# Sample attention gathered ahead of the sample delta rule, mixer loads reordered, last norm's sums given priority

## The chip, the cores and the metric

The kernel runs on one core of one Trainium2 chip. The metric is the time of one execution in device microseconds (us). Five engines work side by side, each through its own list of instructions in order: TensorE (PE, with its weight loads as PEld), VectorE (DVE), ScalarE (ACT), GpSimd (POOL) and SyncE (SP), which here only issues DMAs. An instruction that needs another engine's result, or a transfer, waits at the head of its engine's list, and everything behind it waits too.

## The reference, cut to what matters

One step of one layer serves a prompt of 1024 tokens and, with the same weights, eight sample sequences of four tokens each (`D_MODEL` 1024, float32 throughout):

```python
h = rmsnorm(x, norm_mix_w);  p = h @ w_in            # q,k,v | conv input | z | a | b | gate_A | gate_B
o_a = stick_breaking(q, k, v)      # 8 heads x 64; samples: 256 past keys from the paged cache and 4 new ones
o_b = gated_delta(silu(conv(u)), z, a, b, state)     # 4 heads, 128x128 state
x = x + (sigmoid(g_a) * (o_a @ w_pa) + sigmoid(g_b) * (o_b @ w_pb)) @ w_o
x = x + square(relu(rmsnorm(x, norm_mlp_w) @ w_up)) @ w_down          # D_FF = 4096
y = rmsnorm(x, norm_final_w)
```

Stick-breaking weights are `sigmoid(z_j)` times the product of `1 - sigmoid(z_i)` over the later keys i, with no softmax. For the samples the past keys and values are pages of 128 rows, found through `page_table`: two pages of keys and two of values for each of the eight sequences.

## The kernel before

Everything is kept with features on the partitions (128) and the 1056 tokens (1024 + 32) along the free axis. A float32 product is made of three passes (`dense`, L137 to L139): a high part of the weights with a high part of the data, high with low, low with high. The order of every engine's instructions is fixed when the program is built: a scheduler with a model of times picks, among what is ready, the next instruction of each engine, `tc.high_priority()` moves some forward, and the result is a static list per engine. So PE often has filler between the steps of a chain: the gate projections (`pd_g`, `proj` jobs `g0_j` and `g1_j`), which belong to no chain in this stretch.

The parts that the change touches, in order of time:

- **Sample delta rule** (tiles of pool `dk`): one step of the delta rule for the 32 sample tokens. It is one long chain: conv sums (`cs`), transposes (`dtn`), norms (`drk`, with a power taken on POOL by `rpow`, L114), decays (`pcd`), `dmt`, products with the states (`dks`, two times 64 short matmuls), three rounds of `dy`, the output and its norm (`df`, again `rpow`), and the new states (`dst`), written out by SP from L723.
- **Sample attention** (pool `bk`): for each sequence s POOL gathers two pages of keys into `kg` (L819, two buffers, so that the gather of s + 2 waits until PE has transposed s), PE transposes them (`dkt`, eight transposes) and ACT copies them to `kts`. Four sequences make a group g: scores `dsc`, sigmoid `ds`, the scan on DVE, weights back through transposes `dwt`, values `dav` (from `vg`, gathered at L833, four buffers), `om`, `dos`, `osT`. Group 1 does the same with the other four sequences.
- **Prompt attention** (`sc`, `wt`, `po`): follows; DVE's scans (`pr`) and POOL's `am` and masks feed PE.
- **Channel mixer**: `up_products` (tile `pu`) makes the hidden layer in seven products over blocks of a 2x2 split and writes the combined operands to `hc_d` in DRAM (L1308). The second matrix runs as seven products for three groups of hidden blocks (tile `pw`): for each product i and each block f of a group it needs `hc{f}_i` (264 KB, L1360) and one of the quarters `a11`, `a12`, `a21`, `a22` of `w_down` (256 KB each, L1368) or a combination of them made on DVE, each split into a high and a low part by ACT and DVE. The loads all go through SP's queue: three rounds of `hc`, then all sixteen quarters of the group.
- **Last part** (tile `pv`): the remaining hidden blocks by plain products in four stages of 264 columns (`wd` weights, `hp` hidden), added to `y`; squares of `y` are summed into `sa` (L1484), PE sums over the partitions (`pf`, L1492), POOL takes the power -0.5 (`fr`), PE transposes `y` back (`fin`), ACT and DVE scale one half each (`fo`), and SP writes the rows out. The last stage has three tiles of tokens, the others two.

Of the kernel before, what the change touches and what calls it, by code (L numbers as in the profile page):

```python
# [38 lines left out]
def hybrid_step(ctx, tc, x_prompt, x_sample, cache_k, cache_v, page_table, state_conv, state_ssm,  # L39
# [730 lines left out]
    idx = bk.tile([P, 16], I32, name="idx")  # L770
    nc.scalar.dma_start(idx, page_table.rearrange("s g -> (s g)").unsqueeze(0).to_broadcast([P, 16]))
    rowi = bk.tile([P, 16], I32, name="rowi")
    G.iota(rowi, pattern=[[0, 16]], base=0, channel_multiplier=1)
    V.tensor_scalar(idx, idx, P, None, op0=ALU.mult)
    V.tensor_tensor(idx, idx, rowi, op=ALU.add)
    ckf = cache_k[0].rearrange("n t h d -> (n t) (h d)")
    cvf = cache_v[0].rearrange("n t h d -> (n t) (h d)")

# [32 lines left out]
    vgs = {}  # L811
    for g in range(2):
        psc = ttile(f"dsc{g}")
        kts = []
        for s4 in range(4):
            s = 4 * g + s4
            kg = bk.tile([P, 2, 512], F32, tag="kg", name=f"kg{s}", bufs=2)
            for pg in range(2):
                G.indirect_dma_start(kg[:, pg, :], None, ckf, bass.IndirectOffsetOnAxis(ap=idx[:, 2 * s + pg:2 * s + pg + 1], axis=0))  # L819
            kt = bk.tile([P, 4, 260], F32, tag="kts", name=f"kts{s}", bufs=6)  # L820
            for p2 in range(2):
                pt = (gtile if p2 else dtile)(f"dkt{s}_{p2}")
                for q in range(4):
# [2 lines left out]
                S_.activation(kt[:, 2 * p2:2 * p2 + 2, 0:256], pt.rearrange("p (a f) -> p a f", a=2), AF.Copy)
            V.tensor_copy(kt[:, :, 256:260], ksT[:, :, 4 * s:4 * s + 4])
            kts.append(kt)
        for s4 in range(4):
            s = 4 * g + s4  # L830
            vgs[s] = vk.tile([P, 2, 512], F32, tag="vg", name=f"vg{s}", bufs=4)
            for pg in range(2):
                G.indirect_dma_start(vgs[s][:, pg, :], None, cvf, bass.IndirectOffsetOnAxis(ap=idx[:, 2 * s + pg:2 * s + pg + 1], axis=0))  # L833
# [702 lines left out]
```

## Time and profile before

| | us |
|---|---|
| median of three runs (lowest, highest) | 1775.74 (1774.68, 1777.79) |
| the profiled execution | 1775.13 |
| its span, first to last recorded instruction | 1773.2 |
| outside the span | 1.93 |

| stage by PE's tiles | from, to (us) |
|---|---|
| gate projections used as filler (`pd_g`) | 464.2 to 765.7 |
| key pages transposed (`dkt`) | 548.3 to 643.7 |
| scores of the prompt attention (`sc`) | 681.4 to 879.1 |
| first matrix of the mixer, last matmul of `pu` | 1410.8 |
| second matrix, seven products (`pw`), first matmul | 1416.3 |
| `pv`, end | 1763.0 |
| last instruction of a compute engine, end | 1769.9 |

PE is busy for 1710.3 us of the span (96%), DVE 65%, ACT 44%, POOL 12%. Busy means that an instruction was running by the record; an instruction that waits at the head of its list is idle time of its engine, with the releaser named. "issue" as releaser means that the engine waited for nothing the profile shows. PEclk is the granted TensorE clock, 1.00 being full speed.

### The profile page before, as it was taken

The numbers are of one execution on the slowest core, as the hardware profiler recorded it, in microseconds if no ns is written. First come the engines' busy times: TensorE is split into PE (matmuls) and PEld (weight loads), VectorE is DVE, ScalarE is ACT, GpSimd is POOL, SyncE is SP. The second block draws the span as 40 slices with busy tenths as digits, with TensorE's granted clock in tenths as the row PEclk, the third lists the DMA queues.
The fourth block names the chain that finished last, engine by engine and source line by source line (L and its number), as shares of the span: only waits on it lengthen the run. The fifth ranks groups of instructions, "written<-read, shape, count | busy, mean of one in ns | idle before, by whom it ended". The sixth has DMA issues, their size and how long they took to land.

```text
span 1773.2 us, 34494 instructions
## 1 busy us (share of the span) xinstructions
PE 1710.3 (96%) x13884; PEld 1646.6 (93%) x13884; DVE 1156.5 (65%) x2312; ACT 785.3 (44%) x1563; POOL 205.0 (12%) x239
## 2 busy tenths in 40 slices
PE   7999999999999889999899999999999899999998
PEld 6999999999999668977789999999999899999998
DVE  6665777767234213677947577877777778788853
ACT  5553444343323223566523445555445555434454
POOL 1120111110001322356500000000000000000000
PEclk9999999999999889999999999999999999999999
DMA  5142232234335546578323544645444684432421
GB/s 175 43 119 77 56 115 78 90 104 145 113 106 153 181 133 160 143 186 231 125 96 121 163 145 134 171 140 149 148 141 134 216 303 146 156 112 94 135 84 75
DMA packets 233579, 239.22 MB, mean 135 GB/s; under 512 B 22754, under 2 KB 192067, under 8 KB 233420
## 3 DMA queue, kind: packets, MB, share of 16 engines
q1 hardware_dynamic: 229110, 228.40, 42.2%
q0 software_dynamic: 2560, 8.39, 1.5%
q8 instruction: 109, 1.79, 0.4%
q10 hardware_dynamic: 1750, 0.23, 0.1%
q14 instruction: 50, 0.41, 0.1%
HBM read 163.21 MB, written 73.77 MB: 134 GB/s over the span
## 4 chain that ended last, share of the span: by engine, by line
PE 70%; issue 12%; POOL 6%; DVE 6%; DMA 4%; ACT 1%; SPq 0%; POOLq 0%; DVEq 0%; ACTq 0%; another core or an unknown queue 0%
PE pu L139 6%; PE pu L137 6%; PE pu L138 6%; PE pw L138 5%; PE pw L137 5%; PE pw L139 5%; POOL am L909 3%; POOL s L906 2%; PE px L138 1%; PE px L139 1%; PE pv L137 1%; PE px L137 1%; PE pv L139 1%; PE pv L138 1%; PE pd_g L137 1%
## 5 line engine op out<-in xcount | busy, mean ns | idle before, releaser
L137 PE MATMUL pu<-Xh,uh 128*128 128x264 f32 x812 | 229.8, 283 | 1.0 <-ACT uh L1135 1.0
L139 PE MATMUL pu<-Xh,ul 128*128 128x264 f32 x812 | 230.1, 284 | 0.0
L138 PE MATMUL pu<-Xl,uh 128*128 128x264 f32 x812 | 229.7, 283 | 0.0
L137 PE MATMUL pw<-hc,w 128*128 128x264 f32 x728 | 206.7, 286 | 5.2 <-ACT w L1382 5.2
L138 PE MATMUL pw<-hc,w 128*128 128x264 f32 x728 | 207.0, 287 | 0.0
L139 PE MATMUL pw<-hc,w 128*128 128x264 f32 x728 | 201.7, 284 | 0.0
L137 PEld LDWEIGHTS pu<-Xh,uh 128*128 128x128 f32 x812 | 153.1, 189 | 1.2 <-ACT uh L1135 1.2
L138 PEld LDWEIGHTS pu<-Xl,uh 128*128 128x128 f32 x812 | 152.7, 188 | 0.0
L138 PE MATMUL pd_g<-xl,wh_g 128*128 128x256 f32 (+1 forms) x512 | 149.0, 291 | 3.2 <-issue 3.2
L139 PEld LDWEIGHTS pu<-Xh,ul 128*128 128x128 f32 x812 | 152.0, 188 | 0.0
L137 PE MATMUL pd_g<-xh,wh_g 128*128 128x256 f32 (+1 forms) x512 | 149.8, 293 | 1.4 <-issue 0.8
L139 PE MATMUL pd_g<-xh,wl_g 128*128 128x256 f32 (+1 forms) x512 | 149.9, 293 | 0.3 <-issue 0.3
L137 PEld LDWEIGHTS pw<-hc,w 128*128 128x128 f32 x728 | 137.8, 189 | 5.4 <-ACT w L1382 5.4
L138 PEld LDWEIGHTS pw<-hc,w 128*128 128x128 f32 x728 | 137.5, 189 | 0.0
L139 PEld LDWEIGHTS pw<-hc,w 128*128 128x128 f32 x728 | 135.4, 188 | 0.0
L913 DVE TENSOR_TENSOR_SCAN pr<-am 128x127 f32<-128x127 f32 (+7 forms) x64 | 89.8, 1403 | 43.0 <-POOL am L909 42.9
L138 PEld LDWEIGHTS pd_g<-xl,wh_g 128*128 128x128 f32 x512 | 97.6, 191 | 7.4 <-issue 7.1
L137 PEld LDWEIGHTS pd_g<-xh,wh_g 128*128 128x128 f32 x512 | 97.6, 191 | 6.2 <-issue 4.8
L139 PEld LDWEIGHTS pd_g<-xh,wl_g 128*128 128x128 f32 x512 | 97.5, 190 | 4.8 <-issue 4.6
L1382 ACT ACTIVATE w<-a 128x512 fp32r<-128x512 f32 x78 | 43.4, 623 | 94.3 <-PE pw L139 88.5
L114 POOL TENSOR_TENSOR fr<-fr,powc 128x3 f32<-128x3 f32 x4 | 3.4, 858 | 679.0 <-DVE fr L1493 643.2
L139 PE MATMUL px<-mh,wl_wo 128*128 128x264 f32 x256 | 72.7, 287 | 1.3 <-DVE wl_wo L1136 1.2
(581 smaller groups left out, 5198.7 us busy)
## 6 DMA issues: line engine op xcount, KB each, us to landing
hc_d<-t SPq DMA_DIRECT2D x26, 924.0 KB
hc<-hc_d SPq DMA_DIRECT2D x91, 264.0 KB
a<-in_w_down_dram SPq DMA_DIRECT2D x52, 256.0 KB
ws_g<-in_w_in_dram SPq DMA_DIRECT2D x16, 512.0 KB
ws_wo<-in_w_o_dram SPq DMA_DIRECT2D x32, 256.0 KB
ua<-in_w_up_dram SPq DMA_DIRECT2D x16, 512.0 KB
ub<-in_w_up_dram SPq DMA_DIRECT2D x16, 512.0 KB
gA_d<-gt SPq DMA_DIRECT2D x8, 528.0 KB
```

The source lines that it names most:

```text
L114: G.tensor_tensor(out, in_, powc[: out.shape[0], which:which + 1].to_broadcast([out.shape[0], n]), op=ALU.pow)
L137: PE.matmul(pt[:, :n], lhsT=wh[k], rhs=xh[k], start=(k == 0), stop=False)
L138: PE.matmul(pt[:, :n], lhsT=wh[k], rhs=xl[k], start=False, stop=False)
L139: PE.matmul(pt[:, :n], lhsT=wl[k], rhs=xh[k], start=False, stop=(k == nk - 1))
L906: G.affine_select(s[:, qsl], s[:, qsl], pattern=[[-1, P]], compare_op=ALU.is_gt, fill=0.0, base=0, channel_multiplier=1)
L909: G.tensor_scalar(am[:, :n], s[:, :n], -1.0, 1.0, op0=ALU.mult, op1=ALU.add)
L913: V.tensor_tensor_scan(pr[:, n - 1:0:-1], am_r, am_r, 1.0, op0=ALU.mult, op1=ALU.bypass)
L1382: S_.activation(tl[:, 0], src, AF.Copy)
```

## The change

**Sample attention.** The table of row numbers (`idx`) and the gathers of keys and values come from two helpers, `keys(s)` and `values(s)`. For the first four sequences they are called before the delta rule's code, for the other four inside the loop of group 1. The transposes use PSUM tiles of one kind (`dtile`, two buffers) and no longer of two; `kts` has four buffers and not six, `ds` one and not two; the pool `vk` is gone, `vg` lives in `bk`.

POOL's list, before, from the mask of the delta rule to the first mask of the prompt attention. L819 rows are gathers of keys, L833 of values, two gathers to a row; `drk` and `df` are the delta rule's powers:

```order
L819 DMA kg_6126<-in_cache_k_dram,idx 128x512 x2
L819 DMA kg_6143<-in_cache_k_dram,idx 128x512 x2
L114 TENSOR_TENSOR drk<-drk_4352,powc 128x1
L114 TENSOR_TENSOR df<-df,powc 128x1
L819 DMA kg_6160<-in_cache_k_dram,idx 128x512 x2
L819 DMA kg_6177<-in_cache_k_dram,idx 128x512 x2
L833 DMA vg_6194<-in_cache_v_dram,idx 128x512 x2
L833 DMA vg_6197<-in_cache_v_dram,idx 128x512 x2
L833 DMA vg_6200<-in_cache_v_dram,idx 128x512 x2
L833 DMA vg_6203<-in_cache_v_dram,idx 128x512 x2
L819 DMA kg_6264<-in_cache_k_dram,idx 128x512 x2
L819 DMA kg_6281<-in_cache_k_dram,idx 128x512 x2
```

The same place now (L578 keys, L591 values):

```order
L578 DMA kg_4283<-in_cache_k_dram,idx 128x512 x2
L591 DMA vg_4299<-in_cache_v_dram,idx 128x512 x2
L578 DMA kg_4302<-in_cache_k_dram,idx 128x512 x2
L591 DMA vg_4318<-in_cache_v_dram,idx 128x512 x2
L591 DMA vg_4337<-in_cache_v_dram,idx 128x512 x2
L591 DMA vg_4356<-in_cache_v_dram,idx 128x512 x2
L114 TENSOR_TENSOR drk<-drk_4434,powc 128x1
L578 DMA kg_4321<-in_cache_k_dram,idx 128x512 x2
L578 DMA kg_4340<-in_cache_k_dram,idx 128x512 x2
L578 DMA kg_6261<-in_cache_k_dram,idx 128x512 x2
L578 DMA kg_6277<-in_cache_k_dram,idx 128x512 x2
L578 DMA kg_6293<-in_cache_k_dram,idx 128x512 x2
```

Twelve gathers stand ahead of the power `drk` where four stood. Behind the rows shown come `df`, the last keys (`kg`, two gathers) and the eight gathers of group 1's values.

On PE, before, at the second half of the `dks` products of the delta rule (L675; rows of L137 to L139 are gate projections):

```order
L137 MATMUL pd_g_3_3_8538<-xh_167,wh_g_3_8456 128x288
L138 MATMUL pd_g_3_3_8538<-xl_168,wh_g_3_8456 128x288
L139 MATMUL pd_g_3_3_8538<-xh_167,wl_g_3_8457 128x288
L675 MATMUL dks<-sst,kz_4441 32x128 x32
L137 MATMUL pd_g_3_3_8538<-xh_167,wh_g_3_8456 128x288
L138 MATMUL pd_g_3_3_8538<-xl_168,wh_g_3_8456 128x288
L139 MATMUL pd_g_3_3_8538<-xh_167,wl_g_3_8457 128x288
L137 MATMUL pd_g_3_3_8538<-xh_167,wh_g_3_8456 128x288
```

The same place now, where the transposes of s = 2 and s = 3 lie among the `dks` products (L707):

```order
L137 MATMUL pd_g_3_2_8508<-xh_169,wh_g_3_8452 128x256
L138 MATMUL pd_g_3_2_8508<-xl_170,wh_g_3_8452 128x256
L139 MATMUL pd_g_3_2_8508<-xh_169,wl_g_3_8453 128x256
L707 MATMUL dks<-sst,kz_4523 32x128
L111 MATMUL dkt_0_4325<-ident,kg_4321 128x128 x3
L111 MATMUL dkt_1_4331<-ident,kg_4321 128x128 x3
L707 MATMUL dks<-sst,kz_4523 32x128 x23
L111 MATMUL dkt_0_4344<-ident,kg_4340 128x128 x4
L707 MATMUL dks<-sst,kz_4523 32x128 x3
L111 MATMUL dkt_1_4350<-ident,kg_4340 128x128 x4
L707 MATMUL dks<-sst,kz_4523 32x128 x5
```

The same holds for s = 4, whose transposes follow about twenty PE instructions after those of s = 3; all five sets (s = 0 to 4) now come before the first `dy`. The first score of the prompt attention moves from place 4418 of PE's list to place 4294, so 124 rows fewer lie ahead of it, and that much more of the gate projections lies behind it.

**Second mixer matrix.** Tiles and loads are made in another order. For the first group the first product's four `hc` and the four `a11` are loaded from POOL's queue; the rest goes through SP's queue in the order in which the products need it, tied by `issue_after` (a helper `queued` that makes each load follow the one before), and `y` is loaded in halves at four later points. The sum `s1` moves to product 2. SP's list, before, at the end of the first matrix (L1360 `hc`, L1368 quarters of `w_down`):

```order
L1360 DMA hc_0_16764<-hc_d 128x528
L1360 DMA hc_1_16912<-hc_d 128x528
L1360 DMA hc_1_16916<-hc_d 128x528
L1360 DMA hc_1_16920<-hc_d 128x528
L1360 DMA hc_1_16924<-hc_d 128x528
L1360 DMA hc_2_17060<-hc_d 128x528
L1360 DMA hc_2_17064<-hc_d 128x528
L1308 DMA hc_d<-t_16571 128x7x264
L1360 DMA hc_2_17068<-hc_d 128x528
L1360 DMA hc_2_17072<-hc_d 128x528
L1368 DMA a_3_16720<-in_w_down_dram 128x512
L1368 DMA a_3_16722<-in_w_down_dram 128x512
```

SP's list now:

```order
L1318 DMA hc_d<-t_16567 128x7x264
L1380 DMA a_3_16719<-in_w_down_dram 128x512
L1380 DMA a_4_16724<-in_w_down_dram 128x512
L1380 DMA a_5_16729<-in_w_down_dram 128x512
L1380 DMA a_6_16734<-in_w_down_dram 128x512
L1372 DMA hc_1_16896<-hc_d 128x528
L1372 DMA hc_1_16900<-hc_d 128x528
L1372 DMA hc_1_16904<-hc_d 128x528
L1372 DMA hc_1_16908<-hc_d 128x528
L1318 DMA hc_d<-t_16676 128x7x264
L1468 DMA y_16768<-x_d 128x528
```

and POOL's list beside it:

```order
L114 TENSOR_TENSOR rs_12490<-rs_12490,powc 88x6
L1372 DMA hc_0_16740<-hc_d 128x528
L1372 DMA hc_0_16744<-hc_d 128x528
L1372 DMA hc_0_16748<-hc_d 128x528
L1372 DMA hc_0_16752<-hc_d 128x528
L1380 DMA a_3_16720<-in_w_down_dram 128x512
L1380 DMA a_4_16725<-in_w_down_dram 128x512
L1380 DMA a_5_16730<-in_w_down_dram 128x512
L1380 DMA a_6_16735<-in_w_down_dram 128x512
```

What stands ahead of the first `a11` is now the four `hc` of the first product on POOL's queue, and no longer twelve `hc` on SP's.

**Last part.** The loads of `wd` and of the hidden halves alternate, first half first. In the last norm the last square of each stage stays in a tile of its own, `sl`; PE sums `sa` and `sl` one after the other into the same place, which doubles the `pf` matmuls (9 more float32 matmuls over the four stages), and DVE has four additions fewer. The whole block gets priority, and the third tile of the last stage has PSUM tiles of its own.

```diff
+    vgs, kts_ = {}, {}
+
+    def keys(s):
+        kg = bk.tile([P, 2, 512], F32, tag="kg", name=f"kg{s}", bufs=2)
+        for pg in range(2):
+            G.indirect_dma_start(kg[:, pg, :], None, ckf, bass.IndirectOffsetOnAxis(ap=idx[:, 2 * s + pg:2 * s + pg + 1], axis=0))
+        kt = bk.tile([P, 4, 260], F32, tag="kts", name=f"kts{s}", bufs=4)
+        for p2 in range(2):
+            pt = dtile(f"dkt{s}_{p2}")
...
+        vgs[s] = bk.tile([P, 2, 512], F32, tag="vg", name=f"vg{s}", bufs=4)
...
+    for s in range(4):
+        keys(s)
+        values(s)
     dctx = ExitStack()
     dk = pool("dk", stack=dctx, side="right")
...
     for g in range(2):
         psc = ttile(f"dsc{g}")
-        kts = []
+        if g:
+            for s in range(4, 8):
+                keys(s)
+        kts = [kts_[4 * g + s4] for s4 in range(4)]
         for s4 in range(4):
             s = 4 * g + s4
...
+            V.tensor_copy(kts[s4][:, :, 256:260], ksT[:, :, 4 * s:4 * s + 4])
+            if g:
+                values(s)
...
     for gi, fs in enumerate(groups):
-        qs2 = [load_q(f) for f in fs]
+        qs2 = [quarters(f) for f in fs]
...
+            for n, (q, f) in enumerate(zip(qs2, fs)):
+                if gi == 0 and i < 3:
+                    for nm in (("a11",), ("a12",), ("a21", "a22"))[i]:
+                        if i == 0:
+                            load_part(q, f, nm, G)
+                        else:
+                            queued(lambda: load_part(q, f, nm))
+            for n, f in enumerate(fs):
+                ld = lambda: load_h(hc_d[f - NPL, i], f"hc{f}_{i}", G if gi == 0 and i == 0 else SY)
+                hs[n] = queued(ld) if gi == 0 and i else ld()
...
+        with tc.high_priority():
+            pf = bk2[0](f"pf{c}")
...
+                PE.matmul(pf[:n, i:i + 1], lhsT=sa[:, t * P:t * P + n], rhs=ones[:, 0:1], start=True, stop=False)
+                PE.matmul(pf[:n, i:i + 1], lhsT=sl[:, t * P:t * P + n], rhs=ones[:, 0:1], start=False, stop=True)
...
-                pt = (gtile, ttile)[hf](f"fin{t}_{hf}")
+                pt = (gtile, ttile)[hf](f"fin{t}_{hf}") if i < 2 else dtile(f"fin{t}_{hf}", hf == 1)
```

More of the change, by code (lines that the diff above doesn't have):

```diff
@@ L767, in hybrid_step @@
                     SY.dma_start(dst[p], src)
[L770 to L777, printed above, removed]
     brow = bk.tile([P, 1], F32, name="brow")
@@ L838, in hybrid_step @@
         n = 260
-        ds_ = bk.tile([P, n], F32, tag="ds", name=f"ds{g}", bufs=2)
+        ds_ = bk.tile([P, n], F32, tag="ds", name=f"ds{g}")
         S_.activation(ds_, psc[:, 0:n], AF.Sigmoid, bias=brow, scale=HD ** -0.5)
@@ L1352, in hybrid_step @@
     HD2 = D // 2
+    hq = [None]
     def split2(tl):
@@ L1416, in combine, with queued @@
             add(half(ys[j], 1), acc[2, j])
+    YLOAD = {1: (0, 0), 3: (HJ, 0), 4: (0, 1), 6: (HJ, 1)}
+    last_q = [None]
+    def queued(load, keep_=True):
+        with ExitStack() as st:
+            if last_q[0] is not None:
+                st.enter_context(tc.issue_after(last_q[0].ins))
+            r = load()
+        if keep_:
+            last_q[0] = r if hasattr(r, "ins") else hq[0]
+        return r
     groups = [list(range(3, 7)), list(range(7, 11)), list(range(11, 16))]
     for gi, fs in enumerate(groups):
-        qs2 = [load_q(f) for f in fs]
-        for i in range(7):
-            hs = [load_h(hc_d[f - NPL, i], f"hc{f}_{i}") for f in fs]
+        qs2 = [quarters(f) for f in fs]
+        if gi:
+            for q, f in zip(qs2, fs):
+                for nm in PARTS:
+                    queued(lambda: load_part(q, f, nm), False)
+        for i in range(7):
+            hs, ws = [None] * len(fs), [None] * len(fs)
+            for n, (q, f) in enumerate(zip(qs2, fs)):
[8 more added lines that the diff above has]
+                hs[n] = queued(ld) if gi == 0 and i else ld()
             ws = [weight_part(q, f, i) for q, f in zip(qs2, fs)]
             if gi == 0 and i == 0:
-                for j in range(KT):
-                    ys[j] = fp.tile([P, T], F32, name=f"y{j}")
-                    SY.dma_start(ys[j], x1_d[j])
+                ys[:] = [fp.tile([P, T], F32, name=f"y{j}") for j in range(KT)]
+            if gi == 0 and i in YLOAD:
+                j0, h = YLOAD[i]
+                for j in range(j0, j0 + HJ):
+                    queued(lambda: SY.dma_start(half(ys[j], h), half(x1_d[j], h)))
             for j in range(HJ):
@@ L1453, in hybrid_step @@
     fl = list(range(NPL)) + list(range(NF, NF + NPL))
-    wd = []
-    for f in fl:
-        tl = wlp.tile([P, 2, D], F32R, name=f"wd{f}")
-        for c in range(2):
+    wd = [wlp.tile([P, 2, D], F32R, name=f"wd{f}") for f in fl]
+    hid = [[], []]
+    for c in range(2):
+        for i, f in enumerate(fl):
             cs_ = slice(c * HD2, (c + 1) * HD2)
```

90 lines of the change are left out of this document (43 added, 47 removed).

## The prediction

> **What bounds the kernel now.** I read the page's shares first, then the waits, then windows and timelines where PE is not full.
>
> ```profile
> PE 1710.3 (96%) x13884; PEld 1646.6 (93%) x13884; DVE 1156.5 (65%) x2312; ACT 785.3 (44%) x1563; POOL 205.0 (12%) x239
> ```
>
> PE is the bound: of 1773.2 us some 63 are free, so the change, which removes hardly any PE work, can only win idle or slow PE time back. The windows around the sample attention show where much of that lies (busy us and, in brackets, instructions of PE, PEld, DVE, ACT, POOL; then clock, DMA share, GB/s):
>
> ```profile
> 540.00:560.00 20.00, 19.48 (x210) 18.92 (x209) 8.93 (x26) 11.73 (x21) 4.46 (x5) 1.00 0.54 167
> 600.00:610.00 10.00, 8.68 (x71) 8.11 (x69) 1.42 (x3) 2.23 (x4) 7.56 (x9) 1.00 1.03 328
> 610.00:620.00 10.00, 6.52 (x22) 4.43 (x23) 0.00 (x0) 2.56 (x5) 5.71 (x7) 0.53 0.63 203
> 620.00:630.00 10.00, 10.00 (x89) 8.85 (x90) 3.08 (x8) 2.46 (x5) 1.35 (x2) 0.96 0.39 116
> 630.00:640.00 10.00, 9.05 (x77) 6.40 (x74) 0.14 (x2) 2.68 (x7) 7.21 (x8) 1.00 0.79 224
> 640.00:650.00 10.00, 5.89 (x18) 3.07 (x19) 1.18 (x3) 2.06 (x4) 4.17 (x5) 0.56 0.54 159
> 650.00:660.00 10.00, 10.00 (x87) 8.88 (x87) 1.77 (x6) 2.35 (x5) 0.00 (x0) 0.92 0.01 2
> ```
>
> A full window holds 87 to 89 matmuls. The four others hold 71, 22, 77 and 18, so by count (1 - n/88) x 10 us they lose 1.9, 7.5, 1.3 and 8.0: 18.7 us, in two stalls of about 9.4 (an estimate, since the short products of the sample attention are mixed in). POOL's timeline shows what goes on meanwhile:
>
> ```profile
> 539.81 1.23 POOL L819 DMA_INDIRECT kg<-in_cache_k_dram,idx  x1 [10.08 <-DVE cs L589]
> 543.85 0.95 POOL L819 DMA_INDIRECT kg<-in_cache_k_dram,idx  x1 [0.30 <-issue]
> 546.28 0.58 POOL L114 TENSOR_TENSOR drk<-drk,powc 128x1 f32<-128x1 f32 x1 [1.48 <-DVE drk L620]
> 599.37 1.02 POOL L819 DMA_INDIRECT kg<-in_cache_k_dram,idx  x1 [16.30 <-PE dkt L111]
> 613.23 0.95 POOL L833 DMA_INDIRECT vg<-in_cache_v_dram,idx  x1 [0.30 <-issue]
> 616.94 0.95 POOL L819 DMA_INDIRECT kg<-in_cache_k_dram,idx  x1 [2.76 <-remote]
> 620.70 0.95 POOL L819 DMA_INDIRECT kg<-in_cache_k_dram,idx  x1 [0.30 <-issue]
> 630.65 0.94 POOL L819 DMA_INDIRECT kg<-in_cache_k_dram,idx  x1 [9.00 <-PE dkt L111]
> 634.41 0.95 POOL L819 DMA_INDIRECT kg<-in_cache_k_dram,idx  x1 [0.31 <-issue]
> 644.44 0.95 POOL L833 DMA_INDIRECT vg<-in_cache_v_dram,idx  x1 [0.30 <-issue]
> ```
>
> Gathers start every 1.25 us; there are runs of 4 (539.81, 616.94) and of 12 (599.37, 630.65). PE inside the two long runs:
>
> ```profile
> 609.46 0.28 PE L137 MATMUL pd_g<-xh,wh_g 128*128 128x256 f32 x1 [0.60 <-issue]
> 615.11 0.37 PE L138 MATMUL pd_g<-xl,wh_g 128*128 128x256 f32 x1 [1.72 <-issue]
> 638.46 0.60 PE L111 MATMUL dkt<-ident,kg 128*128 128x128 f32 x4
> 641.41 1.89 PE L872 MATMUL dos<-sel,om 128*128 128x16 f32 x8 [2.36 <-DVE om L869]
> 648.50 1.08 PE L836 MATMUL dsc<-kts,qbd 128*32 128x260 f32 x2 [0.88 <-ACT kts L826]
> ```
>
> Filler that waits for nothing trickles from 609 to 617, and from 639 to 649 every signal comes late. Both stalls begin 8 to 9 us after the run's first gather and end, by the last of these rows and the full window from 620, some 3.5 us after its last. That fits the short runs too: 5 us are over before 9 have passed, and they show no gap. So I price a run of gathers of length L at L - 8.7 + 3.5 us, and never below nothing. DMA share does not decide it: the second stall ran at 0.54 to 0.79.
>
> **The change part by part.** The sum goes against the profiled execution, 1775.13 us, 0.6 under the median of 1775.74.
>
> *Stalls.* The first twelve gathers now form one run ahead of `drk` (15 us), and the last group's values a run of eight (10 us). By the formula they cost 9.8 and 4.8, so of 18.7 about 4.1 are won. The bounds: a win of all 18.7 if it is not the run as such that stalls, and a loss of 6 if the next key gathers join on and the first run becomes 16 (20 us, 14.8). I take 4.1, since both long runs seen did stall. What hides the gathers' own time is filler on PE.
>
> *New waits.* With two `kg` buffers, s + 2 is gathered only after s is transposed: two gathers, 2.5 us, then landing (the last key gather ends at 635.4 and its transposes run by 638.46: up to 3.1), up to 5.6 us in all. Between s = 2 and s = 4 PE has some twenty rows, 2.3 us at the filler's 0.114 (88 in 10 us); the wait there is up to 3.3, those for s = 2 and 3 are 0 to 2 each. I take 3 (0 to 7). Behind the twelve gathers waits `drk`: ready at 546.28 before, now at about 555.4. DVE's `ds1` needs it, and the copy of `dmt` stands behind that; PE needs this copy only for the first `dy`, so 12 us of cover remain, and it costs nothing while these hold; past them every further us falls on the chain.
>
> ```profile
> 568.03 0.38 PE L685 MATMUL dy<-dr__4475,dMT 128*128 128x128 f32 x2
> ```
>
> *Filler.* The prompt attention's first score stands 124 PE rows earlier, about 15 us, and so much filler lasts longer into it.
>
> ```profile
> 681.00:766.00 85.00, 83.99 (x672) 75.82 (x672) 51.19 (x49) 41.88 (x95) 29.45 (x48) 1.00 0.50 132
> 766.00:840.00 74.00, 66.37 (x523) 53.10 (x522) 58.49 (x56) 49.97 (x112) 46.97 (x51) 0.95 0.92 241
> ```
>
> With filler PE idles 1%, without it 10%. Filler of 15 us stretched over some 20 us of attention saves about 2 (0 to 7.6, the idle time of the second row).
>
> *Mixer.* The transition now:
>
> ```profile
> 1410.77 0.28 PE L139 MATMUL pu<-Xh,ul 128*128 128x264 f32 x1
> 1416.27 0.59 PE L137 MATMUL pw<-hc,w 128*128 128x264 f32 x1 [5.22 <-ACT w L1382]
> 1419.52 0.29 PE L137 MATMUL pw<-hc,w 128*128 128x264 f32 x1
> 1396.80 6.93 SPq L1360 DMA_DIRECT2D hc<-hc_d  x10
> 1407.69 12.81 SPq L1368 DMA_DIRECT2D a<-in_w_down_dram  x17
> 1415.60 0.62 ACT L1382 ACTIVATE w<-a 128x512 fp32r<-128x512 f32 x1
> 1400.00:1410.00 10.00, 10.00 (x85) 10.00 (x84) 7.70 (x17) 8.13 (x14) 0.00 (x0) 1.00 1.03 361
> ```
>
> The gap is 5.4 us, and the next matmuls up to 1419.52 come every 0.22 instead of 0.12, 1.5 more: 6.9. The engines move 361 GB/s at a share of 1.0, so bytes ahead of the first `a11` count. Now these are 4 x 264 and 4 x 256 KB, 2.1 MB: 5.9 us alone, 11.8 if SP's queue takes half. The first `hc` start at 1396.80 as buffers come free; allowing 2 us for the other order of the buffers, the data is there between 1404 and 1411, and with the split (0.62 on ACT, about as much on DVE) the first product can go at 1406 to 1413. PE is done with `pu` at 1410.9. I take 1412.5 with 1 us of slow clock: 4.4 won (0 to 6.9). An issue on POOL costs PE nothing unless eight of them act like a run of gathers: 10 us, 4.8, which would just undo this.
>
> *Last part.* PE's waits at its start, and its end:
>
> ```profile
> PE pv L137 <- DVE y L1478: 0.7, 1, 0.7
> PE pv L137 <- ACT wd L1461: 0.6, 1, 0.6
> 1764.65 0.76 PE L1492 MATMUL pf<-ones,sa 128*128 128x1 f32 x6
> 1765.34 0.44 PE L111 MATMUL fin<-ident,y 128*128 128x128 f32 x2
> 1767.45 1.71 PE L111 MATMUL fin<-ident,y 128*32 128x128 f32 x8 [1.68 <-ACT fo L1505]
> 1769.20 0.74 DVE L1507 TENSOR_SCALAR fo<-fin,fr 32x512 f32<-32x512 f32 x1 [1.08 <-PE fin L111]
> ```
>
> Interleaved loads win 0.5 of the 1.3 (0 to 1.3). Six `pf` passes take 0.69, 0.115 each; nine more float32 matmuls are 18 passes, 2.1 us, of which the 12 passes of the first three stages, 1.4 us, go straight onto PE's dense path. At the tail `fr` comes some 1.3 later (six more passes, and the third tile's transposes ahead of them), but `fo` then runs through without the wait of 1.68 and ends near 1770.1 instead of 1769.94. Together +1.5 (0.8 to 2.2). The four DVE additions saved lie beside PE and are worth nothing.
>
> The sum: 1775.1 - 4.1 + 3 - 2 - 4.4 - 0.5 + 1.5 = **1768.6**.
>
> **Rivals.** *The stalls go* (0.28). They may need what else stood at 600 to 650: state writes, transposes that free one gather pair at a time, PE's chain behind each signal. For it speaks that the early part is loaded otherwise; against it, that the two stalls are alike at DMA shares of 1.03 and 0.79. Then 18.7 are won in place of 4.1, and the waits shrink to 2: 1753.
>
> *The stalls move whole* (0.12). If PE trickles for a reason other than the run of gathers, all 18.7 stay wherever this work stands: 1768.6 + 4.1 = 1772.7. The windows speak for a tie to the runs of 12, two times out of two. The Trainium skill's page "SBUF — State Buffer", section "Who interferes with whom", would side with this rival: it holds that a DMA never contends with a compute engine. In this trace the trickling matmuls at 609 to 617 without a wait speak against applying it here.
>
> *Slower* (0.15). The transposes of s = 2 to 4 now stand in PE's list inside the delta rule, and a signal in a stall came 8 to 15 us late:
>
> ```profile
> ACT kts L826 <- remote: 23.3, 2, 15.0
> ```
>
> If the early stall catches two round trips from PE to POOL and back (transposed, gathered, transposed), each 8.3 us late (23.3 - 15.0) with the chain of `dks` behind them, 16.6 stand in place of 3: 1782. It decides the sign from the point where these waits pass 9.5 us, 3 + 6.5.
>
> **How the numbers follow.** The forecast has 0.45, with a range of its own of 1762 to 1775; the rivals 0.28, 0.12 and 0.15. A measurement tells 0.2% (3.6 us) from no change. Faster: 0.37 of the first, all 0.28, 0.05 of the third, together 0.70; same 0.06 + 0.05 + 0.01 = 0.12; slower 0.18. The range of 8 in 10 reaches from just under the case without stalls to a part of the slow one: 1751 to 1778.
>
> **What would show it.** Right: PE trickling or late signals around 548 to 558 and again near the eight value gathers, 14 to 15 us lost by count; a first `pw` matmul within 3 us of the last `pu`; `pf` with 36 passes; little idle time of PE until some 20 us later than 766 in the prompt attention. Wrong: windows of 85 or more matmuls throughout 545 to 680 (the first rival); waits of PE for `kg` DMAs of over 10 us before the first `dy` (the last); `pw` still starting at 1416. The weakest step is the formula for the stalls, drawn from four runs of gathers.

## The result, and the profile after

Beside each other on one chip, the kernel before took 1778.61 us (median, 1774.68 to 1783.38) and the changed one 1763.44 (1760.95 to 1771.33): a ratio of 0.9919 with an interval of 0.9904 to 0.9934, some 14.4 us less. The forecast was 1768.6, which is 6.5 less than the profiled execution of before that it was reckoned from (1775.13).

The two profiled executions are not typical of these: that of before (1775.13 us) is one of its fastest, that of after (1765.93 us, a span of 1764.2) one of its slower ones. So the traces differ by 9.0 us of span where the medians differ by 15.2, and what follows divides up the 9.0; the other 6 lie outside this pair of traces. By the first and last matmul of each stage, the part up to the end of the prompt attention's output product took 969.6 us in place of 977.6 (8.0 less); `pu` 432.9 in place of 433.2; the gap from `pu` to `pw`, from the start of one matmul to the start of the next, 2.7 in place of 5.5; `pw` 268.9 in place of 267.7; `pv` 78.8 in place of 78.9; and from there to the end 11.3 in place of 10.3. The sum is -8.0 - 0.3 - 2.8 + 1.2 - 0.1 + 1.0 = -9.0.

The page's shares of the changed kernel, and the waits of PE that touch the change (waiting operation, what it waited for: us in all, times, longest):

```profile
PE 1706.9 (97%) x13902; PEld 1645.0 (93%) x13902; DVE 1156.2 (66%) x2308; ACT 783.2 (44%) x1563; POOL 204.5 (12%) x247
```

```profile
PE pw L137 <- ACT w L1394: 2.4, 1, 2.4
...
PE dkt L111 <- ACT kts L585: 0.3, 1, 0.3
...
PE pv L137 <- ACT wd L1502: 0.2, 1, 0.2
PE pv L139 <- DVE wd L1503: 0.2, 1, 0.2
```

PE has 18 more matmuls, the second `pf` pass for each tile. No wait of `dkt` for a key gather is among those of any size.

**Sample attention.** POOL's timeline shows the first run of twelve gathers and the run of eight values:

```profile
542.42 1.20 POOL L578 DMA_INDIRECT kg<-in_cache_k_dram,idx  x1 [10.41 <-DVE qbd L830]
...
556.64 0.95 POOL L591 DMA_INDIRECT vg<-in_cache_v_dram,idx  x1 [0.30 <-issue]
557.61 0.60 POOL L114 TENSOR_TENSOR drk<-drk,powc 128x1 f32<-128x1 f32 x1
...
621.96 0.96 POOL L591 DMA_INDIRECT vg<-in_cache_v_dram,idx  x1 [4.49 <-PE dav L875]
...
631.59 0.95 POOL L591 DMA_INDIRECT vg<-in_cache_v_dram,idx  x1 [0.30 <-issue]
```

The windows around them (busy us and, in brackets, instructions of PE, PEld, DVE, ACT, POOL; then the granted clock, DMA share, GB/s):

```profile
540.00:550.00 10.00, 7.98 (x59) 7.54 (x58) 6.39 (x15) 5.56 (x9) 6.06 (x6) 0.92 1.01 314
550.00:560.00 10.00, 7.82 (x57) 7.52 (x56) 0.98 (x7) 2.99 (x7) 6.44 (x9) 0.91 0.79 244
560.00:570.00 10.00, 9.04 (x117) 7.82 (x116) 4.63 (x16) 4.83 (x11) 4.72 (x4) 1.00 0.60 182
546.00:548.00 2.00, 0.55 (x3) 0.31 (x3) 1.27 (x1) 1.97 (x3) 1.39 (x3) 1.00 1.08 371
558.00:560.00 2.00, 0.51 (x5) 0.68 (x5) 0.43 (x2) 0.23 (x3) 0.28 (x2) 1.00 0.93 319
630.00:640.00 10.00, 8.77 (x66) 7.27 (x69) 1.76 (x5) 2.05 (x6) 1.94 (x3) 1.00 0.48 165
```

Short products stand among the filler here, so a count of matmuls misleads. As the measure of a loss I take a window's idle PE time plus (1 - clock) times its busy time; the clock is rounded to hundredths, so this is good to 1 or 2 us. For before, the windows from 600 to 660 quoted in the prediction give 1.3 + 6.5 + 0.4 + 0.95 + 6.7 + 0.8 = 16.7 (by count, 18.7), and as one window 18.4:

```profile
600.00:660.00 60.00, 50.14 (x358) 39.74 (x357) 7.59 (x22) 14.35 (x29) 26.01 (x28) 0.83 0.56 172
```

Nearly half of that, 0.17 x 50.14 = 8.5, is not idle time but the lower clock granted during and after the stalls. For after the first three rows of the view above give 2.7 + 2.9 + 1.0 = 6.5, and the last one 1.2. So 16.7 became some 7.7: 9.0 less, of which 8.0 arrive at the end of this part. (Over the same stretches in both, 540 to 580 and 600 to 660, the measure has 18.9 and 9.0.)

The two short rows show where the early loss lies: around 546 to 548, four to six microseconds into the run, and again from 556 to 560. Some 3.6 of the 6.5 lie around the first, where 1.15 us are a plain wait of PE for ACT (`gt`). The second has the look of the stalls before, filler that waits for nothing (duration, engine, line, operation; in the bracket the idle time ahead):

```profile
557.39 0.38 PE L138 MATMUL pd_g<-xl,wh_g 128*128 128x256 f32 x1 [0.46 <-issue]
559.49 0.28 PE L139 MATMUL pd_g<-xh,wl_g 128*128 128x256 f32 x1 [1.72 <-issue]
...
632.05 0.38 PE L138 MATMUL pd_g<-xl,wh_g 128*128 128x256 f32 x1 [0.23 <-issue]
633.47 0.39 PE L137 MATMUL pd_g<-xh,wh_g 128*128 128x256 f32 x1 [0.43 <-issue]
```

**Mixer.** The transition, from PE and from ACT and POOL:

```profile
1402.51 0.28 PE L139 MATMUL pu<-Xh,ul 128*128 128x264 f32 x1
1405.19 0.59 PE L137 MATMUL pw<-hc,w 128*128 128x264 f32 x1 [2.40 <-ACT w L1394]
...
1408.60 0.28 PE L138 MATMUL pw<-hc,w 128*128 128x264 f32 x1
```

```profile
1401.84 0.65 ACT L1309 ACTIVATE t<-t 128x528 f32<-128x528 f32 x1 [4.57 <-DVE t L1305]
...
1403.97 0.64 ACT L1310 ACTIVATE t<-t 128x528 f32<-128x528 f32 x1
1404.52 1.14 ACT L1394 ACTIVATE w<-a 128x512 fp32r<-128x512 f32 x2
...
1393.02 2.17 POOL L1380 DMA_DIRECT2D a<-in_w_down_dram  x4
```

POOL issues the four `a11` 12 us ahead of the first product, and no wait for them is recorded. What is left of the gap is ACT: four activations of the last `t` tiles (the first and the last of them are shown) stand ahead of the first `w`, at 1404.52, and ACT sat idle for 4.57 us ahead of them, waiting for DVE. The slow clock after the gap is still there: the next matmuls up to 1408.60 come every 0.22 us.

**Last part.** The three last tiles, then the write:

```profile
1757.79 2.05 DVE L1553 TENSOR_SCALAR fo<-fin,fr 128x512 f32<-128x512 f32 x3 [1.05 <-POOL fr L114]
1758.60 1.64 SPq L1554 DMA_DIRECT2D out_dram<-fo  x3
```

`fo` now runs through without the wait that stood before its last tile, and the last computation ends 1759.84, 6.9 us after `pv` (before: 7.0). But the span ends 4.4 us after that, in place of 3.3. By the DMA view the three writes move their 1.18 MB from about 1759.4 to 1762.5, and before from about 1768.2 to 1771.5: 3.1 to 3.3 us in both, but now they start some 0.4 us ahead of the end of the last computation, and before 1.7 ahead.

### The profile page after: what moved, and what is told of

It is laid out like the page before. It is cut to its first block, busy times and chain, and to the rows that moved or that the text cites. A ratio compares the mean times of both kernels' runs of the same rounds, so it can differ in the third digit from the quotient of the medians.

```text
span 1764.2 us, 34556 instructions
## 1 busy us (share of the span) xinstructions
PE 1706.9 (97%) x13902; PEld 1645.0 (93%) x13902; DVE 1156.2 (66%) x2308; ACT 783.2 (44%) x1563; POOL 204.5 (12%) x247
## 4 chain that ended last, share of the span: by engine, by line
PE 79%; DVE 7%; DMA 7%; ACT 2%; issue 2%; POOL 1%; another core or an unknown queue 1%; SPq 1%; DVEq 0%; POOLq 0%; ACTq 0%
PE pu L139 6%; PE pu L137 6%; PE pu L138 6%; PE pw L139 4%; PE pw L138 4%; PE pw L137 4%; PE pd_g L137 3%; PE pd_g L139 3%; PE pd_g L138 3%; PE po L951 2%; PE wt L111 1%; PE px L138 1%; PE px L139 1%; PE px L137 1%; PE pv L137 1%
## 5 line engine op out<-in xcount | busy, mean ns | idle before, releaser
L137 PE MATMUL pu<-Xh,uh 128*128 128x264 f32 x812 | 230.0, 284 | 0.6 <-ACT uh L1145 0.6
L139 PE MATMUL pu<-Xh,ul 128*128 128x264 f32 x812 | 230.1, 284 | 0.0
L137 PE MATMUL pw<-hc,w 128*128 128x264 f32 x728 | 205.6, 285 | 2.4 <-ACT w L1394 2.4
L139 PE MATMUL pw<-hc,w 128*128 128x264 f32 x728 | 201.9, 285 | 0.2 <-DVE w L1395 0.2
L137 PEld LDWEIGHTS pu<-Xh,uh 128*128 128x128 f32 x812 | 153.2, 189 | 1.2 <-ACT uh L1145 1.2
L139 PEld LDWEIGHTS pu<-Xh,ul 128*128 128x128 f32 x812 | 152.0, 188 | 0.0
L137 PE MATMUL pd_g<-xh,wh_g 128*128 128x256 f32 (+1 forms) x512 | 150.2, 293 | 1.6 <-ACT gt L983 1.1
L139 PE MATMUL pd_g<-xh,wl_g 128*128 128x256 f32 (+1 forms) x512 | 149.7, 292 | 1.7 <-issue 1.7
L137 PEld LDWEIGHTS pw<-hc,w 128*128 128x128 f32 x728 | 137.9, 190 | 2.8 <-ACT w L1394 2.6
L139 PEld LDWEIGHTS pw<-hc,w 128*128 128x128 f32 x728 | 134.9, 188 | 0.4 <-DVE w L1395 0.4
L137 PEld LDWEIGHTS pd_g<-xh,wh_g 128*128 128x128 f32 x512 | 97.7, 191 | 7.0 <-issue 4.1
L139 PEld LDWEIGHTS pd_g<-xh,wl_g 128*128 128x128 f32 x512 | 97.8, 191 | 4.3 <-issue 3.7
L139 PE MATMUL px<-mh,wl_wo 128*128 128x264 f32 x256 | 72.7, 287 | 1.3 <-DVE wl_wo L1146 1.2
L138 PE MATMUL px<-ml,wh_wo 128*128 128x264 f32 x256 | 72.6, 285 | 0.0
```

What stands on the lines that cost most here:

```text
L137: PE.matmul(pt[:, :n], lhsT=wh[k], rhs=xh[k], start=(k == 0), stop=False)
L138: PE.matmul(pt[:, :n], lhsT=wh[k], rhs=xl[k], start=False, stop=False)
L139: PE.matmul(pt[:, :n], lhsT=wl[k], rhs=xh[k], start=False, stop=(k == nk - 1))
```

## The experiments

Each was timed beside the kernel before on the same chip. There were three such sets, on three chips, and the kernel before had a median of 1781.8 us in the first, 1762.96 in the second and 1761.74 in the third. That difference is taken up at the end; ratios are compared only within a set.

### The three parts alone

*samp* is the kernel before with the gathers, key transposes and their tables moved as in the change, and nothing else:

```diff
+    for s in range(4):
+        keys(s)
+        values(s)
     dctx = ExitStack()
...
-            kg = bk.tile([P, 2, 512], F32, tag="kg", name=f"kg{s}", bufs=2)
...
+        if g:
+            for s in range(4, 8):
+                keys(s)
```

> Only the sample attention's part of the change, the rest as before. Theory (the two stalls shrink and the prompt attention starts earlier): this part carries most of the gain, ratio to the kernel before 0.992 to 0.996 (7 to 14 us), with the second key gathers' stall gone and a first stall of 5 to 8 us at 549 to 560. Rival, as the prediction priced the parts: this part gives only 3 us, 0.998, and the mixer more than it.

*mix* has the second mixer matrix's loads alone:

```diff
-        qs2 = [load_q(f) for f in fs]
+        qs2 = [quarters(f) for f in fs]
...
+                if gi == 0 and i < 3:
+                    for nm in (("a11",), ("a12",), ("a21", "a22"))[i]:
+                        if i == 0:
+                            load_part(q, f, nm, G)
```

> Only the second mixer matrix's loads and order changed. Theory: the gap between the first and the second matrix falls from 5.4 to about 2.5 us and the slow clock after it stays, so 2 to 4 us in all, ratio 0.998. Rival (the part carries the gain that the sample attention did not): 6 us or more, 0.9965 or less. A gap that is set by ACT's order and not by the loads shows as a wait of PE for ACT with the loads landed before.

*last* has the last part alone: the order of `wd` and `hid`, `sl`, and the priority of `pf`:

```diff
-        pf = bk2[0](f"pf{c}")
+        with tc.high_priority():
+            pf = bk2[0](f"pf{c}")
...
+                PE.matmul(pf[:n, i:i + 1], lhsT=sl[:, t * P:t * P + n], rhs=ones[:, 0:1], start=False, stop=True)
```

> Only the last part changed: loads of the plain weights interleaved, last squares summed by PE, priority for the norm. Prediction: 1.0 us slower (+1.5 for the added passes and the tail, -0.5 for the loads), ratio 1.0006. Rival: priority pays, 1 us faster, 0.9994. With the spread of the runs the trace decides: time from the last product of the second matrix to the end, 89.2 us in the kernel before.

Measured in the first set: samp 0.9911 (0.9886 to 0.9936), mix 0.9973 (0.9955 to 0.9991), last 0.9990 (0.9973 to 1.0007). Times 1781.8 that is -15.9 us, -4.8 (-8.0 to -1.6) and -1.8 (-4.8 to +1.2). The sample part carries most of the gain, a little more than was expected of it (0.992 to 0.996). The windows from 600 to 660, of samp, mix and last in turn, and of samp at its early run:

```profile
600.00:660.00 60.00, 58.34 (x475) 47.18 (x475) 12.58 (x30) 14.60 (x31) 10.41 (x10) 1.00 0.60 167
540.00:580.00 40.00, 34.70 (x334) 30.61 (x332) 14.56 (x39) 15.93 (x29) 21.68 (x21) 0.91 0.65 205
```

```profile
600.00:660.00 60.00, 51.05 (x374) 41.90 (x374) 7.94 (x22) 14.59 (x29) 26.52 (x28) 0.86 0.57 176
```

```profile
600.00:660.00 60.00, 48.71 (x344) 38.49 (x343) 7.16 (x20) 13.61 (x28) 26.55 (x28) 0.83 0.61 184
```

Where the gathers stand as before, the stalls stand as before: 16.1 us lost in mix (8.95 idle, 0.14 x 51.05 by the clock) and 19.6 in last. In samp 1.7 is left there, and 8.4 is found at the early run (5.3 idle, 0.09 x 34.7). So the stall moves with the run of twelve, and about half of it is gone. With the early stretch of mix and last counted too (1.2 and 3.6), 7 to 13 us are won by this measure; the timed -15.9 is more, with an interval down to -11.4 and a profiled execution (1771.17) that is among samp's slowest.

### Does a run of gathers stall PE by itself?

*probe* is the kernel before with added gathers from `cache_k` in its first mixer matrix, where PE is full and neither the sample attention nor its chain is near. Nothing uses the data. They go into six reused slots of 128 x 512, chained, each block behind a different `f`: 8 gathers, 12, 16, then 12 plain transfers of the same bytes issued by POOL, 12 gathers again, and 12 gathers with four small POOL operations after each:

```diff
+    PROBE = {4: ("g", 8), 6: ("g", 12), 8: ("g", 16), 10: ("p", 12), 12: ("g", 12), 14: ("x", 12)}
+        for i in range(n):
+            with tc.issue_after(last.ins):
+                if kind in "gx":
+                    last = G.indirect_dma_start(dst[:, i % 6, :], None, pf_, bass.IndirectOffsetOnAxis(ap=pidx[:, i:i + 1], axis=0))
+                    if kind == "x":
+                        for _ in range(4):
+                            last = G.tensor_scalar(pjk[:, 32:64], pjk[:, 32:64], 1.0, 0.0, op0=ALU.mult, op1=ALU.add)
+                else:
+                    last = G.dma_start(dst[:, i % 6, :], pf_[i * P:(i + 1) * P, :])
```

> The kernel before with idle gathers added in the first mixer matrix, where POOL is otherwise empty and PE runs one dense product after the other: at six blocks, runs of 8, 12 and 16 gathers back to back, 12 plain transfers issued by POOL, 12 gathers again, and 12 gathers with four small POOL instructions (about 1.2 us) between each two. Theory (the run of gathers as such starves PE): PE trickles from 8 to 9 us after a run's first gather until 3 us after its last, losing about 5, 10 and 15 us in the first three and 10 in the fifth, less or none in the spaced one. Rival (the stall needs the state writes and the chain of short PE steps of the sample attention): no window of the first matrix loses over 1 us, and the time is that of before within 3 us.

The windows, in the blocks' order (first gather of each block at 1160.92, 1223.34, 1270.42, the plain transfers at 1321.31, then 1362.32 and 1410.04):

```profile
1170.00:1180.00 10.00, 10.00 (x84) 10.00 (x83) 7.87 (x16) 6.68 (x13) 1.53 (x2) 1.00 0.68 209
1223.00:1233.00 10.00, 10.00 (x84) 10.00 (x83) 7.56 (x16) 3.73 (x7) 7.52 (x8) 1.00 0.72 240
1230.00:1240.00 10.00, 6.55 (x43) 5.58 (x42) 3.34 (x7) 2.66 (x5) 6.76 (x7) 0.89 0.89 283
1240.00:1250.00 10.00, 10.00 (x67) 10.00 (x67) 5.60 (x14) 3.84 (x8) 0.00 (x0) 0.77 0.59 193
1280.00:1290.00 10.00, 7.68 (x47) 6.02 (x45) 2.86 (x5) 3.38 (x6) 7.78 (x8) 0.95 0.96 298
1290.00:1300.00 10.00, 8.41 (x37) 7.58 (x37) 4.02 (x11) 1.29 (x2) 1.10 (x2) 0.54 0.57 195
1330.00:1340.00 10.00, 10.00 (x85) 10.00 (x84) 5.28 (x12) 3.39 (x6) 0.55 (x1) 1.00 0.94 311
1370.00:1380.00 10.00, 8.31 (x57) 7.78 (x56) 5.03 (x10) 4.17 (x8) 6.91 (x7) 0.89 0.92 300
1420.00:1430.00 10.00, 10.00 (x84) 10.00 (x84) 5.29 (x14) 4.04 (x7) 8.34 (x21) 1.00 0.86 289
```

A full window has 84.5 matmuls of one kind here, so a count is exact enough. This is one execution. Eight gathers cost PE nothing. Twelve cost 4.9 + 2.1 = 7.0 us the first time and about 3.8 the second (3.3 + 0.5; the window from 1380 has 80). Sixteen cost 4.4 + 5.6 = 10.0. Twelve plain transfers of the same size, at 311 GB/s and a DMA share of 0.94, cost nothing, and neither do twelve gathers with pauses. The losses add up to 20.8, and the first matrix as a whole is 21.7 longer than in before (454.9 in place of 433.2). A part is again the clock: from 1240 to 1250 PE is busy throughout, at 0.77, with 67 matmuls. Inside the first run of twelve:

```profile
1234.78 0.38 PE L146 MATMUL pu<-Xl,uh 128*128 128x264 f32 x1 [0.46 <-issue]
1236.18 0.28 PE L147 MATMUL pu<-Xh,ul 128*128 128x264 f32 x1 [1.02 <-issue]
```

So a long unbroken run of indirect gathers starves PE, on this chip, with nothing to wait for, from some 10 to 11 us after the first gather (nothing is lost up to 1233) until some 2 us after the last (1237.68). What went on around 600 to 650 is not needed for it. The plain transfers are not a full counterpart: POOL issued the twelve in 9.3 us (1321.31 to 1330.62), no longer than the eight gathers that cost nothing, so the kind of transfer and the length of the run aren't told apart. The prediction's formula (a run of L us costs L - 8.7 + 3.5, with 10, 15 and 20 us for 8, 12 and 16 gathers) says 4.8, 9.8 and 14.8; measured are 0, then 7.0 and 3.8, then 10.0. L - 8.7 alone, 1.3, 6.3 and 11.3, comes nearer: the formula takes the whole duration of a stall as lost, and PE trickles in it and does not stand still. It is no law either: for the two runs in the kernel before it gives 12.6, and they lost 16.7.

### Number of gathers, or bytes?

Two readings were left: a queue of outstanding bytes (A), or the number of gathers issued without a break (B). *probe2* uses gathers of a quarter of a row (16 and 12 of them), eight and then a pause and four more, ten, and twelve with one small operation between:

```diff
-    PROBE = {4: ("g", 8), 6: ("g", 12), 8: ("g", 16), 10: ("p", 12), 12: ("g", 12), 14: ("x", 12)}
+    PROBE = {4: ("q", 16), 6: ("p", 12), 8: ("g", 10), 10: ("x", 12), 12: ("q", 12)}
+                if kind == "q":
+                    last = G.indirect_dma_start(dst[:, i % 6, 0:P], None, pq_, bass.IndirectOffsetOnAxis(ap=pidq[:, i:i + 1], axis=0))
```

> Again gathers added in the quiet first mixer matrix, at five blocks: 16 back to back with rows of a quarter of the size (512 B, as many rows), 8 + 4 with a pause of about 3.6 us of small POOL instructions between, 10 back to back, 12 with one small POOL instruction between each two, 12 back to back of quarter rows. Theory A (too many gathers outstanding because their bytes drain slower than they are issued): the quarter rows lose nothing, the pause and the run of 10 lose under 2 us. Theory B (the number of gathers or rows issued in a row, whatever their size): 16 quarter rows lose about 10 us as 16 whole ones did, 12 lose 4 to 8; the pause helps all the same.

The window of the ten gathers, and the run of values and keys in the sample attention of the same trace:

```profile
1250.00:1268.00 18.00, 18.00 (x149) 18.00 (x148) 14.00 (x31) 7.92 (x15) 11.26 (x10) 1.00 0.84 260
...
590.00:630.00 40.00, 38.29 (x301) 31.76 (x300) 5.81 (x16) 12.35 (x24) 26.92 (x28) 0.96 0.83 258
```

None of its blocks lost anything. That would speak for A, but the last row forbids it: on this chip the sample attention, left as it was, loses 1.7 + 0.04 x 38.3 = 3.2 us where it lost 16 to 20 on the first. And these 3.2 are not the stall. Between 538 and 662 PE has no idle time without a releaser here; what it waits for most is the data of key gathers:

```profile
PE dkt L121 <- DMA kg<-in_cache_k_dram,idx: 1.7, 2, 1.2
```

The six traces of the first comparison and the first set (before, after, samp, mix, last, probe) have 4.3 to 10.0 us of idle time without a releaser in that stretch; the seven of the second and third sets have none. The stall is absent here, so this run tells nothing of its cause. A and B stay open.

### Runs broken up

*bpause* is the kernel before with its gathers chained and twelve small POOL operations after the eighth gather of each run of twelve; *apause* is the changed kernel with its gathers as pairs and such pauses so that no run is over eight:

```diff
+    def pause(k=12):
+        for _ in range(k):
+            chained(lambda: G.tensor_scalar(pzk, pzk, 1.0, 0.0, op0=ALU.mult, op1=ALU.add))
...
+            if s4 == 1:
+                pause()
```

> The kernel before, nothing moved ahead; only a pause of about 3.6 us of small POOL instructions put into each of its two runs of twelve gathers, after the eighth. Theory (the runs of twelve are what stalled PE, and ending them is what the change won): the two stalls fall from about 18 to 0 to 4 us, ratio to the kernel before 0.990 to 0.994. Rival (the gain comes from where the work stands, ahead of the delta rule and the prompt attention earlier): the stalls stay or come back as waits for values, 0.998 to 1.002.

> The changed kernel with its twelve first gathers issued as eight, a pause, four, a pause, four, and the last eight values as four, a pause, four. Theory: the rest of the stall at 549 to 570 (about 6 us by count of matmuls) goes, ratio to the kernel before 0.988 (0.992 for the change itself), if the later values and keys cost no wait. Rival: what is left there is the chain of PE, gathers and back and not the run, so 0.992 or more.

Measured in the second set: bpause 1.0002 (0.9987 to 1.0018), apause 0.9976 (0.9966 to 0.9987). In bpause the windows are full:

```profile
600.00:660.00 60.00, 59.23 (x491) 49.54 (x489) 9.71 (x24) 17.42 (x36) 32.78 (x52) 1.00 0.61 194
```

0.8 us are lost in 60, and still no time is won, on a chip where there was no stall to win: probe2's 3 us are waits for gathers and clock, and bpause's interval (-2.3 to +3.2 us) excludes a win of 3. In apause `dkt` waited 3.1 us in all for its keys, which its expectation had left as a condition. Breaking the runs where the stall is large was not tried, so whether it alone would bring what the move brought there stays open.

### The rest of the mixer's gap

*whi* is the changed kernel with the first copy of `w` on POOL in place of ACT; *best* also takes its subtraction from DVE to POOL:

```diff
-        S_.activation(tl[:, 0], src, AF.Copy)
+        if eng is not None:
+            eng.tensor_copy(tl[:, 0], src)
+            eng.tensor_tensor(tl[:, 1], src, tl[:, 0].bitcast(F32), op=ALU.subtract)
+            return tl
+        S_.activation(tl[:, 0], src, AF.Copy)
```

> The changed kernel, but the high part of the first product's four weights of the second matrix made by POOL and no longer by ACT, whose list has the last two activations of the first matrix ahead of it. Theory (the gap of 2.7 us that is left is ACT's order, the data has landed): first product within 1 us of the last one of the first matrix, 1.5 to 2.5 us faster than the change, ratio 0.991. Rival (the weights land late): the gap stays at 2 us or more with POOL waiting for the loads.

> The changed kernel with both parts of the first product's four weights of the second matrix made by POOL. With the high parts alone on POOL the gap went to 0.3 us but PE then waited 3.6 us for DVE's low parts. Theory: these waits go as well, 3 to 4 us faster than the changed kernel, ratio to it 0.998. Rival: POOL takes too long for eight operations and PE waits for it instead, no faster than the changed kernel.

whi: 0.9973 (0.9955 to 0.9990) in the second set; best: 0.9972 (0.9959 to 0.9985) in the third. In both the gap is gone, 0.1 us. But `pw` takes 271.4 us in whi and 272.1 in best in place of 268.9, so gap and `pw` together are 271.5 and 272.2, and 271.6 in the changed kernel. The waits of whi and of best show where it went:

```profile
PE pw L139 <- DVE w L1398: 3.6, 2, 2.3
```

```profile
PE pw L138 <- DVE hc L1368: 2.4, 1, 2.4
```

And a window of best there:

```profile
1415.00:1420.00 5.00, 2.55 (x21) 2.33 (x20) 5.00 (x11) 4.83 (x9) 0.00 (x0) 1.00 1.05 400
```

DVE is busy without a break (the window from 1420 to 1425 is alike) and the DMA engines are at a share of 1.05: after the first products, splits and transfers are the limit, and an earlier first product only waits later.

### The same kernels once more, and everything together

*after_b* is the changed kernel, unaltered, and *bpause_b* is bpause, unaltered; *bestp* is best with the pauses of apause.

> The changed kernel once more, since the kernel before took about 1781 us on the chip of the first four experiments and 1763 on that of the second four, and the stalls were smaller on the latter. Theory (the change wins the stalls, and their size is the chip's): where the kernel before takes 1775 or more, ratio 0.990 to 0.994; where it takes about 1763, 0.996 to 0.999, the mixer's 2 to 4 us and little else. Rival (the gain does not hang on the stalls): 0.992 on any chip.

> The kernel before with its runs of twelve gathers broken by a pause, once more, beside the change on the same chip. Theory: where the kernel before takes 1775 or more, 0.990 to 0.995, near what the change gives; where it takes about 1763, 1.000 again. Rival (moving the work is what wins): 0.998 or more on a chip where the kernel before is slow.

> The same with the changed kernel's long runs of gathers broken by pauses as well. Theory: where the stalls are large, 4 to 6 us faster than without the pauses; where they are small, the same or 1 us slower, since PE then waits up to 3 us for keys.

In the third set: after_b 0.9975 (0.9961 to 0.9988), bpause_b 1.0017 (1.0000 to 1.0034), best as above, bestp 0.9986 (0.9973 to 0.9999). Here the whole change is worth 4.4 us (2.1 to 6.9) in place of 14.4, within what was expected for a chip where the kernel before takes about 1763. Windows of after_b, then of best, whose sample part is the same code:

```profile
540.00:580.00 40.00, 36.03 (x368) 33.28 (x367) 17.31 (x43) 17.23 (x31) 23.91 (x23) 0.96 0.70 215
```

```profile
540.00:580.00 40.00, 37.98 (x396) 35.29 (x395) 17.20 (x40) 17.40 (x32) 25.13 (x23) 1.00 0.75 233
```

The early stretch loses 5.4 us in one and 2.0 in the other. That is not the stall either: PE's waits there have releasers, ACT (1.6 and 0.2) and the data of the key gathers, in after_b and then in best:

```profile
PE dkt L111 <- DMA kg<-in_cache_k_dram,idx: 2.4, 2, 1.9
```

```profile
PE dkt L111 <- DMA kg<-in_cache_k_dram,idx: 1.8, 3, 1.0
```

Within the third set no kernel beat the changed one by more than the intervals: best stands at 0.9972 beside its 0.9975, and pauses on top of best gave nothing. apause (0.9976) and whi (0.9973) belong to the second set, in which the changed kernel was not timed.

## Why the prediction was right or wrong

The sign and the range held, and 1763.4 lies within the forecast's own 1762 to 1775. The size of the win did not hold: 6.5 us were forecast and 14.4 measured. That the time still comes within 5.2 us of the forecast is in part luck, since the kernel before took 1778.6 in this comparison and not the 1775.1 of the sum. Step by step, from the two profiled executions:

*Stalls (-4.1).* The place was right in the main and the cause held on this chip: filler trickles without a wait at 557 to 560 and at 632 to 634, behind the last gathers of the two runs, and the added gathers in the quiet stage show that the run itself does it. The size was wrong. The term "9.8 and 4.8" measured 6.5 and 1.2, and not all of the 6.5 belongs to it: the 3.6 around 546 to 548 come four to six microseconds after the first gather, earlier than the formula has any, and are in part a wait for ACT. The step that failed is the price of a run, which took a stall's whole duration, 3.5 us behind the last gather included, as lost; a run of eight proved free in the quiet stage. In after, and more closely in samp, four key gathers follow right behind `drk` (from 559.93 and 560.47), so the first run comes near the 16 that the prediction named as a bound, at 14.8, and it cost 6.5 and 8.4. So 9.0 went in place of 4.1, about half of the loss, and so the truth lies between the forecast and the first rival, "the stalls go" (1753).

*New waits (+3).* They did not come in this pair; the wait of `dkt` above is 0.3 us. In the third set they did: `dkt` waits 2.4 us for its keys in after_b, near the 3 of the sum, and 1.8 in best. `drk` ran at 557.61 (expected: 555.4), and the first `dy` at 580.95, 12.9 us later than before, within the filler's cover. The rival "slower", late signals on the way from PE to POOL and back, had its mechanism in part. This row of DVE in the stall shows it:

```profile
559.57 0.16 DVE L668 COPY dcg<-pcd 128x2 f32<-128x2 f32 x1 [8.99 <-remote]
```

DVE was idle for 9 us there. PE had written the last `pcd` by 554.2, so the signal came some 5.4 us late, where the kernel before has under 0.1 (548.45 and 548.49). PE had filler meanwhile, so the price was not paid. In the same way the 15.0 us that the prediction read as lateness count from the end of ACT's work before; the transposes it waited for ran only from 636.5 on, so some 10 of them were lateness.

*Filler into the prompt attention (-2).* The first score came 20.7 us earlier (660.7, before 681.4) and filler lasted 11.6 longer (777.4, before 765.8), not 20. It won little: in the windows from 760 to 920, of before and of after, PE is busy about as long.

```profile
760.00:920.00 160.00, 146.15 (x1160) 122.25 (x1159) 120.58 (x140) 88.08 (x193) 75.21 (x84) 0.98 0.60 169
```

```profile
760.00:920.00 160.00, 144.28 (x1162) 121.58 (x1162) 113.34 (x133) 78.31 (x174) 61.71 (x70) 1.00 0.58 163
```

With the clock counted, 16.8 are lost in the one and 15.7 in the other. What failed is that filler would cover the later attention too: over the whole of it PE's waits of `wt` for DVE's `s` rose from 3.9 us (4 times) to 9.2 (6 times). The three terms together, -3.1, measured -8.0.

*Mixer (-4.4).* The first `pw` came 2.7 us behind the last `pu`, within the 3 named as the sign. But the gap shrank by 2.8 only; the slow clock behind it stayed, as it was to do in part; and `pw` in this pair is 1.2 longer. So the pair has -1.6. Over the traces gap and `pw` together are 273.2 to 275.0 us with the old loads (before, samp, last, bpause, bpause_b) and 271.2 to 271.6 with the new (mix, after, apause, after_b), a difference of 2.7 on the average. The step that failed is the first product at 1412.5 with 1 us of slow clock: the bytes were there, but ACT stood behind four `t` activations, which the sum had not counted, and the slow clock cost as much as before.

*Last part (-0.5 and +1.5, together +1.0).* The traces have +0.9, right by accident. PE's waits at the start of `pv` fell from 1.3 (0.7 of it for `y`, 0.6 for `wd`) to 0.4, as forecast or better. `pv` was not lengthened by the 1.4 us of mid passes: 78.8 in place of 78.9. The microsecond was lost where the sum had nothing, from the last computation to the end: 4.4 us in place of 3.3; the time from the end of `pv` to the end of the span is 11.3 in all traces with this part. The sum had followed `fo` and not the writes behind it, which start later against the end of the computation, as the times above show. The run of this part alone could not tell it from nothing.

*The rival "the stalls move whole"* (1772.7) fell: the stall moved, but not whole. As to the rule named beside it, from the Trainium skill's page "SBUF — State Buffer", section "Who interferes with whom", that a DMA never contends with a compute engine: plain transfers at 311 GB/s agree with it (85 matmuls in the window), twelve indirect gathers on the first set's chip do not (43), though by what way they slow PE is open.

## What to carry to other kernels

Where a matmul stream trickles without a wait, look for a long unbroken run of indirect gathers on POOL beside it; on the chip where that showed, runs of eight and runs with small POOL operations between cost nothing. Breaking runs up was timed only on chips without the stall, where it won nothing. Time such a change on more than one chip: this one was worth 0.8% in its first comparison and 0.25% in another, with the same code. And where a gap is closed at a place at which transfers and the engines that split the data are full, look for the same time a few microseconds later before counting it as won.
